# Chunks 2 and 3 of the gated up-projection: from two ordinary products each to a first seven-product pair that shares its time with the making of the sums of x

## The chip, the core and the metric

The kernel runs on one core of one Trainium2 chip. The metric is the device time of one execution in microseconds (us), from the kernel's start to its end. All matrices are fp32; the matrix engine works on them as pairs of a rounded high part (fp32r) and the rest, its low part, so one product of two fp32 matrices is three matrix multiplications: high by high, high by low, low by high.

Engines, as the profile names them: PE (matrix multiplications), PEld (its weight loads), ACT (ScalarE), DVE (VectorE), POOL (GpSimd), SP (it only issues DMAs here). Each takes its instructions in the order in which the program gives them, so an instruction that waits holds up all that stand behind it on its engine.

## The reference

Two decoder layers over x (512 tokens of 1024 features). Each layer has an attention part and then a gated feed-forward part; only the latter is touched:

```python
def conv_ffn(xn, w_up, cw, cb, w_down):        # xn: (1, 512, 1024), w_up: (1024, 5632)
    a = xn @ w_up
    T = a.shape[1]
    ap = jnp.pad(a, ((0, 0), (CONV_W - 1, 0), (0, 0)))
    a = sum(ap[:, j:j + T] * cw[j] for j in range(CONV_W)) + cb
    gate, val = jnp.split(a, 2, axis=-1)
    return (jax.nn.gelu(gate, approximate=True) * val) @ w_down
...
f = conv_ffn(rms_norm(h, g[2]), w_up[l], conv_w[l], conv_b[l], w_down[l])
h = h + rms_norm(f, g[3])
```

w_up has 2816 gate columns and 2816 value columns: 22 chunks of 128 of each. A chunk c is finished by three conv taps on gate and value, a GELU and a product.

## The kernel before

The function `ffn` (line 616) does one layer's feed-forward part, with x transposed (features on the partitions, 512 tokens along the row) and split in high (`xT[0]`, two tiles of four feature blocks) and low (`xT[1]`). It is written as one sequence of calls; that sequence is the order on every engine. There is no other scheduler. Its parts in the up-projection:

- `first_products` (L544) makes chunks 0 and 1 (four outputs "first"): the first half of the tokens (LO) for all four while the last two token blocks are still being normed and transposed (`bd.transpose`, L359 to L367), then the second half (HI).
- `sums_in` (L656) makes sums of quarters of x. POOL adds high and low to whole x in two instructions (L660), DVE makes four differences (L662, L663, L665, L666), and ACT and DVE split the results in high (`xsh`, L671) and low (`xsl`, L672). The first tile of sums is called XA, the second XB. It is a generator: each `next` gives out one step.
- Chunks 2 and 3 are ordinary: `up` (L963) multiplies a piece of 1024 x 128 weights by all 512 tokens, 24 matmuls of 512 columns; gate and value of two chunks are four such pieces, 96 matmuls.
- Chunks 4 to 19 go in eight pairs of chunks (class `Pair`, L678, and the loop at L1020). A pair's 1024 x 256 block of gate or value weights is cut in quarters A11, A12, A21, A22, and by Strassen's scheme in the form of Winograd the pair's eight quarter products become seven, of 24 matmuls of 256 columns each: p_1 (A11 by x itself), p_2 (A12 by x), p_3 (S4 by x), p_4 (A22 by XB), p_5 (S1 by XA), p_6 (S2 by XB) and p_7 (S3 by XA). The sums of weights are S1 = A21 + A22, S3 = A11 - A21, S2 = S1 - A11 and S4 = A12 - S2 (`add`, L686, on DVE). The eighth, needless product is what is saved. In the loop a pair's order on PE is p_7, p_6, p_4, p_5, then p_1 of the next pair, then p_2, p_3.

An operand of weights is split by `high` (L703): ACT copies the high part (L705); then either `low` (L710) lets DVE subtract (S2, S3, S4), or, with `added`, ACT also writes the negated weights, rounded the same way (L707), and a DMA that POOL issues adds the raw weights onto them (L708), which leaves the low part. PE multiplies the low weights as the third matmul of each group of three (L288, L289, L290 in `mm3`), so it stops there if the low part is late.

`keep` (L725) copies partial results out of PSUM on ACT, `Chunk.tap` (L632) runs the conv taps on ACT (L623) and DVE (L624, L625), `gelu` is L643, `product` L645. Weights come by SP's queue in the order of the list `pieces` (L150), made by `add_ffn` (L182); `W.ahead` and `W.ahead_dma` say how many pieces ahead are split and loaded.

Before the change, the program stands after `first_products` as: POOL's two additions, taps of chunk 0, the differences, product of chunk 0, taps of chunk 1, chunk 2's two products with the splitting of the sums, S1 and S3 beside them, chunk 3's two products with S2, S4 and A22, then p_1 of pair 4 and the loop.

Of the kernel before, what the change touches and what calls it, by code (L numbers as in the profile page):

```python
# [13 lines left out]
ALU = mybir.AluOpType  # L14
# [4 lines left out]
KD = D // 128  # L19
HD = 64  # L20
DFF = 2816
# [3 lines left out]
BIG = 3.0e38  # L25


PAIRS = tuple(range(4, 20, 2))
ND = NF // 2
LAST = 3  # L30

# [84 lines left out]
def trunk_kernel(ctx, tc, x, norm_gains, w_qkv_a, w_o_a, w_q_b, w_o_b, kv_norm, w_kvf, b_f,  # L116
# [11 lines left out]
    def t8(shape, dt=F32, name="t8"):  # L128
        return p8.tile(shape, dt, tag="t8", name=name)
# [52 lines left out]
    def add_ffn(l):  # L182
        for c in range(NF):
            if c in PAIRS:
                for q, f in ((0, 0), (0, DFF), (1, DFF), (1, 0)):
                    add_block(w_up[l], q, f + c * 128)
            elif c - 1 not in PAIRS:
                add_cols(w_up[l], c * 128)
                add_cols(w_up[l], DFF + c * 128)

        for j in range(ND):
            add(lambda raw, j=j: [(raw[:, 0:512], w_down[l][j * 256:j * 256 + 128, 0:512]),
                                  (raw[:, 512:1024], dT[l][j, :, 0:512])])
            add(lambda raw, j=j: [(raw, dT[l][j, :, 512:1536])])
        add_rows(w_down[l], range(1, NF, 2))
# [345 lines left out]
                self.out(b)  # L541


    def first_products(bd, n):  # L544
        bd.norm(3)
        outs = [bank([128, T], name="first") for _ in range(n)]
        ws = []
        for i, o in enumerate(outs):
            ws.append(W.get())
            feat_mm(ws[i], bd.xT, o, LO)  # L550
            if i == 0:
                bd.transpose(2)
            if i == 2:
                bd.transpose(3)
        for w, o in zip(ws, outs):
            feat_mm(w, bd.xT, o, HI)
        return outs
# [58 lines left out]
    def ffn(l, bd, cp, nxt, gain, ahead):  # L616
# [39 lines left out]
        def sums_in():  # L656

            v = [t8([128, 4, T], name=f"xsum{i}") for i in range(2)]
            for i in range(2):
                pool.tensor_tensor(v[i], xT[0][i].bitcast(F32), xT[1][i].bitcast(F32), ALU.add)  # L660
            yield
            dve.tensor_tensor(v[0][:, :, LO], v[0][:, :, HI], v[0][:, :, LO], ALU.subtract)  # L662
            dve.tensor_tensor(v[0][:, :, HI], v[1][:, :, HI], v[0][:, :, HI], ALU.subtract)  # L663
            yield
            dve.tensor_tensor(v[1][:, :, HI], v[1][:, :, HI], v[0][:, :, LO], ALU.subtract)  # L665
            dve.tensor_tensor(v[1][:, :, LO], v[1][:, :, LO], v[1][:, :, HI], ALU.subtract)  # L666
            yield
            for X, src in ((XA, v[0]), (XB, v[1])):
                X += [t8([128, 4, T], F32R, name="xsh"), t8([128, 4, T], F32R, name="xsl")]
                for k in (0, 2):  # L670
                    act.copy(X[0][:, k:k + 2], src[:, k:k + 2])  # L671
                    dve.tensor_tensor(X[1][:, k:k + 2], src[:, k:k + 2], X[0][:, k:k + 2].bitcast(F32), ALU.subtract)  # L672
                    yield
# [211 lines left out]
        def run(steps):  # L885
            for _ in steps:
                pass
# [78 lines left out]
                bh, bl = xs(xT, kc, ALL)  # L966
                mm3(o, wh[:, kc, :], wl[:, kc, :], bh, bl, kc == 0, kc == KD - 1)

        base = W.n_get
        first = first_products(bd, 4)  # L970
        xT = bd.xT
        extra = sums_in()
        next(extra)
        done, last = Chunk(0, first[0:2]), Chunk(1, first[2:4])
        done.taps()
        next(extra)
        done.product()
        last.taps()
        W.ahead, W.ahead_dma = 1, 3
        W.split(base + 7)  # L980
        W.high_added()
        pairs = [Pair(c) for c in PAIRS]
        p, n = pairs[0:2]

        banks = p.new_banks()
        up(W.get(), banks[0], range(KD))
        for _ in range(3):
            next(extra, None)
        p.take("A11", "A21", "A22")
        p.high("A11", True)  # L990
        p.s1()
        p.s3()
        up(W.get(), banks[1], range(KD))
        run(extra)
        p.high("S1", True)
        done, last = last, Chunk(2, banks)

        banks = p.new_banks()
        up(W.get(), banks[0], range(KD))
        done.product()  # L1000
        last.tap(0)
        p.high("S3")
        p.s2()
        last.tap(1)
        p.high("S2")
        last.gelu()
        p.take("A12")
        p.low("S3")
        p.s4()
        up(W.get(), banks[1], range(KD))  # L1010
        p.high("A22", True)
        p.low("S2")
        last.product()
        n.take("A11")
        n.high("A11", True)
        p.p_1()
        p.keep_1()
        prev, m = None, [Chunk(3, banks)]

        for i, p in enumerate(pairs):  # L1020
            W.n_get += 4
# [3 lines left out]
            if prev:  # L1025
                prev.sum_1()
            a.tap(0)
            p.high("A12", True)
            p.keep_7()
            p.p_6()  # L1030
            a.tap(1)
            if n:
                n.take("A21", "A22")
                n.s1()
            else:
                W.high_added()
# [25 lines left out]
                b.gelu()  # L1062
            if n:
                n.high("S1", True)
            p.p_2()
            if n:
                n.s2()
            if prev:
# [17 lines left out]
            prev, m = p, p.chunks()  # L1086
# [820 lines left out]
```

## Time and profile before

| what | value |
|---|---|
| device time, median of 3 runs | 1103.73 us (1103.61 to 1103.82) |
| the profiled execution's own time | 1104.32 us |
| its span, first to last instruction | 1102.5 us |
| mean granted PE clock | 0.998 |
| DVE busy | 892.3 us (81%) |
| ACT busy | 735.1 us (67%) |
| POOL busy | 231.5 us (21%) |

Layer 0's feed-forward part begins with `first_products` at 178.0 us of the span, layer 1's at 759.8 us. A row of the timeline gives the start, the length, engine, line, operation, output and inputs with buffer numbers left out, the shape, how many equal instructions are merged (x2), and in brackets how long the engine had been idle and what ended that. A row of the windows gives a stretch, and each engine's busy time in it with the number of instructions that touch it. Pipelined instructions overlap a little, so what one costs in a row is the distance from its start to the next start.

### The profile page before, as it was taken

How to read it: one execution, taken by the hardware profiler on the slowest of the kernel's cores; microseconds unless marked ns; L12 is line 12 of the kernel's file. 1: busy time of each engine (PE TensorE's matmuls, PEld its weight loads, DVE VectorE, ACT ScalarE, POOL GpSimd, SP SyncE). 2: the span in 40 equal slices, each digit the busy share in tenths (PEclk: the TensorE clock that was granted, in tenths of full speed). 3: DMA queues.
4: the chain of work that ended last, by engine and by line, in shares of the span. 5: the costliest groups of instructions: out<-in, count | busy, mean ns of one | idle time of the engine just before them, and what ended most of it. 6: DMA issues, size and time to landing. Idle time of an engine off the chain costs nothing.

```text
span 1102.5 us, 18986 instructions
## 1 busy us (share of the span) xinstructions
PE 1093.6 (99%) x6905; PEld 968.5 (88%) x6905; DVE 892.3 (81%) x1453; ACT 735.1 (67%) x1232; POOL 231.5 (21%) x335
## 2 busy tenths in 40 slices
PE   9999999999999999999999999999999999999997
PEld 6988889899999988888878888889999999988886
DVE  5897788967887789997698677868967887789994
ACT  6754575777788766576562588856677787856572
POOL 2632001322122211000000545600412122211000
PEclk9999999999999999999999999999999999999999
DMA  9699855499999999793447666783499999998872
GB/s 325 184 356 410 317 174 151 91 227 231 224 224 248 230 295 325 277 338 101 134 153 268 210 159 169 216 265 117 98 224 231 231 221 247 224 296 313 317 249 76
DMA packets 156006, 252.06 MB, mean 229 GB/s; under 512 B 12352, under 2 KB 99384, under 8 KB 155912
## 3 DMA queue, kind: packets, MB, share of 16 engines
q1 hardware_dynamic: 137576, 186.61, 51.1%
q0 software_dynamic: 18336, 64.24, 26.3%
q8 instruction: 54, 0.88, 0.3%
q14 instruction: 40, 0.33, 0.1%
HBM read 166.08 MB, written 39.63 MB: 187 GB/s over the span
## 4 chain that ended last, share of the span: by engine, by line
PE 85%; issue 9%; DVE 2%; ACT 2%; DMA 1%; POOL 1%; DVEq 0%; SPq 0%; POOLq 0%; ACTq 0%
PE up L288 12%; PE up L289 12%; PE up L290 12%; PE acc L288 8%; PE acc L290 8%; PE acc L289 8%; PE qk_ps L289 2%; PE qk_ps L288 2%; PE qk_ps L290 2%; PE s_ps L1733 2%; PE o_ps L1781 2%; PE pT_ps L1766 1%; PE first L290 1%; PE first L288 1%; PE first L289 1%
## 5 line engine op out<-in xcount | busy, mean ns | idle before, releaser
L288 PE MATMUL up<-xsh,w 128*128 128x256 f32 x512 | 144.9, 283 | 0.0
L289 PE MATMUL up<-xsl,w 128*128 128x256 f32 x512 | 144.9, 283 | 0.0
L290 PE MATMUL up<-xsh,w 128*128 128x256 f32 x512 | 144.9, 283 | 0.0
L288 PE MATMUL acc<-w 128*128 128x512 f32 (+1 forms) x311 | 120.7, 388 | 0.3 <-DVE mix L337 0.3
L290 PE MATMUL acc<-w 128*128 128x512 f32 (+1 forms) x311 | 120.6, 388 | 0.1
L705 ACT CAST w<-wraw 128x1024 fp32r<-128x1024 f32 x80 | 82.6, 1048 | 37.7 <-DVE wraw L689 37.7
L624 DVE SCALAR_TENSOR_TENSOR bb<-up,conv,bb 128x511 f32<-128x511 f32 x80 | 59.8, 748 | 57.2 <-ACT bb L623 57.0
L289 PE MATMUL acc<-w 128*128 128x512 f32 (+1 forms) x267 | 103.2, 387 | 0.0
L288 PEld LDWEIGHTS up<-xsh,w 128*128 128x128 f32 x512 | 98.3, 192 | 0.0
L289 PEld LDWEIGHTS up<-xsl,w 128*128 128x128 f32 x512 | 98.3, 192 | 0.0
L290 PEld LDWEIGHTS up<-xsh,w 128*128 128x128 f32 x512 | 98.3, 192 | 0.0
L623 ACT ACTIVATE bb<-up,conv 128x512 f32<-128x512 f32 x80 | 60.2, 780 | 32.7 <-DVE up L775 24.3
L288 PE MATMUL up<-xbh,w 128*128 128x256 f32 (+1 forms) x256 | 80.0, 312 | 0.1
L288 PE MATMUL up<-xch,w 128*128 128x256 f32 (+1 forms) x256 | 80.0, 312 | 0.1
L289 PE MATMUL up<-xbl,w 128*128 128x256 f32 (+1 forms) x256 | 79.2, 310 | 0.0
L289 PE MATMUL up<-xcl,w 128*128 128x256 f32 (+1 forms) x256 | 79.2, 310 | 0.0
L290 PE MATMUL up<-xbh,w 128*128 128x256 f32 (+1 forms) x256 | 79.2, 309 | 0.0
L290 PE MATMUL up<-xch,w 128*128 128x256 f32 (+1 forms) x256 | 79.2, 309 | 0.0
L708 POOL DMA_DIRECT2D w<-wraw x48 | 40.4, 841 | 183.5 <-ACT w L707 96.5
L76 DVE TENSOR_TENSOR w<-wraw,w 128x1024 fp32r<-128x1024 f32 x48 | 65.0, 1376 | 11.9 <-ACT w L58 11.4
L58 ACT CAST w<-wraw 128x1024 fp32r<-128x1024 f32 x62 | 63.7, 1051 | 15.8 <-PE v_ps L289 6.9
L290 PEld LDWEIGHTS acc<-w 128*128 128x128 f32 x311 | 58.4, 188 | 12.9 <-DVE w L817 0.9
(308 smaller groups left out, 3279.6 us busy)
## 6 DMA issues: line engine op xcount, KB each, us to landing
wraw<-in_w_up_dram SPq DMA_DIRECT2D x88, 512.0 KB, 6.6
w<-wraw POOLq DMA_DIRECT2D x62, 512.0 KB, 7.6
dT<-dsums SPq DMA_DIRECT2D x28, 512.0 KB, 7.5
dsums<-in_w_down_dram SPq DMA_DIRECT2D x22, 512.0 KB, 7.5
dsums<-in_w_down_dram SPq DMA_DIRECT2D x44, 256.0 KB, 6.6
hD<-hc POOLq DMA_DIRECT2D x44, 256.0 KB, 7.3
wraw<-dT SPq DMA_DIRECT2D x22, 512.0 KB, 6.8
dact<-hD SPq DMA_DIRECT2D x44, 256.0 KB, 5.3
```

The lines of the kernel that those rows point to most:

```text
L58: self.nc.scalar.copy(pair[:, 0], raw)
L76: self.nc.vector.tensor_tensor(pair[:, 1], raw, pair[:, 0].bitcast(F32), ALU.subtract)
L288: pe.matmul(o, ah, bh, start=first, stop=False, skip_group_check=shared)
L289: pe.matmul(o, ah, bl, start=False, stop=False, skip_group_check=shared)
L290: pe.matmul(o, al, bh, start=False, stop=last, skip_group_check=shared)
L623: act.activation(bb[:, s, :], ps, AF.Identity, bias=cp[:, 3, ch:ch + 1], scale=cp[:, 2, ch:ch + 1])
L624: dve.scalar_tensor_tensor(bb[:, s, 1:], ps[:, :T - 1], cp[:, 1, ch:ch + 1], bb[:, s, 1:], ALU.mult, ALU.add)
L705: act.copy(w[:, 0], self.f[key])
L708: pool.dma_start(w[:, 1], self.f[key], accum_op=ALU.add)
L1733: pe.matmul(s[hh][:, :nn], qT[j][:, m, hh, i * 128:(i + 1) * 128], k, start=m == 0, stop=m == 1)
L1766: pe.transpose(o[:, k0 + k, :], p[:, hh, k * 128:(k + 1) * 128], ident)
L1781: pe.matmul(o[64 * hh:64 * hh + 64, i * 128:(i + 1) * 128], Vt[hd // 8][:, k, (hd % 8) * 64:(hd % 8) * 64 + 64], pT[j, i, hh][:, k, :], st ...
```

## The change

`PAIRS` now begins with 2: chunks 2 and 3 become a ninth pair in each layer, and `add_ffn` lists that pair's quarters as A11, A12, A21, A22 (the other pairs keep A11, A21, A22, A12). The four pieces of 96 matmuls of 512 columns become seven products, 168 matmuls of 256 columns. The order around them is rewritten:

- `first_products` splits no weights ahead any more. After the second output it calls `begin`, which takes A11 and A12 and gives out A11's splitting.
- `sums_in` makes XB's two differences only after XA is split.
- After `first_products`: POOL's additions, then A12's splitting, S1 and S3 on DVE, taps of chunk 0, S3's high part, S2, XA's differences, product of chunk 0, p_1, S3's low part, XA's splitting, S2's high part, XB's differences and splitting, S2's low part, p_2, keep_1. Chunk 1's taps move into the loop, to the first pair.
- In the loop the first pair has no p_2 between the next pair's p_1 and its own p_3, gives out A22 and S4 after the first tap, and S1 and the next pair's A11 after the second.

```diff
-PAIRS = tuple(range(4, 20, 2))
+PAIRS = tuple(range(2, 20, 2))
...
-                for q, f in ((0, 0), (0, DFF), (1, DFF), (1, 0)):
+                blocks = (0, 0), (0, DFF), (1, DFF), (1, 0)
+                for q, f in blocks if c > PAIRS[0] else (blocks[0], blocks[3], *blocks[1:3]):
...
             if i == 0:
+                W.ahead, W.ahead_dma = 1, 2
                 bd.transpose(2)
+            if i == 1:
+                begin()
...
-            dve.tensor_tensor(v[1][:, :, HI], v[1][:, :, HI], v[0][:, :, LO], ALU.subtract)
-            dve.tensor_tensor(v[1][:, :, LO], v[1][:, :, LO], v[1][:, :, HI], ALU.subtract)
-            yield
             for X, src in ((XA, v[0]), (XB, v[1])):
+                if src is v[1]:
+                    dve.tensor_tensor(src[:, :, HI], src[:, :, HI], v[0][:, :, LO], ALU.subtract)
+                    dve.tensor_tensor(src[:, :, LO], src[:, :, LO], src[:, :, HI], ALU.subtract)
+                    yield
...
+        pairs = [Pair(c) for c in PAIRS]
+        p = pairs[0]
+
+        def begin():
+            p.take("A11", "A12")
+            p.high("A11", True)
+
+        first = first_products(bd, 4, begin)
         xT = bd.xT
-        extra = sums_in()
-        next(extra)
+        sums = sums_in()
+        next(sums)
+        p.high("A12", True)
+        p.take("A21", "A22")
+        p.s1()
+        p.s3()
         done, last = Chunk(0, first[0:2]), Chunk(1, first[2:4])
         done.taps()
...
+        p.high("S3")
+        p.s2()
+        next(sums)
+        done.product()
+        p.p_1()
+        p.low("S3")
+        for _ in range(2):
+            next(sums)
+        p.high("S2")
+        for _ in range(3):
+            next(sums)
+        p.low("S2")
+        p.p_2()
+        p.keep_1()
+        W.ahead_dma = 3
+        prev, m = None, [last]
...
             a.tap(0)
-            p.high("A12", True)
+            if prev:
+                p.high("A12", True)
+            else:
+                p.high("A22", True)
+                p.s4()
             p.keep_7()
             p.p_6()
             a.tap(1)
+            if not prev:
+                p.high("S1", True)
+                n.take("A11")
+                n.high("A11", True)
...
-            p.p_2()
+            if prev:
+                p.p_2()
```

The program's order on two engines shows the moves. All rows are of layer 0; the changed kernel's line numbers are four or five higher. First DVE after the last block of x has been split (`xbl1`): before, the rows from there to chunk 1's first tap. `w_2104` is a weight of chunk 3, `first_1988` and `first_1989` are chunk 0's gate and value, `xsum0` and `xsum1` are the two tiles of sums.

```order
L367 TENSOR_TENSOR xbl1_1861<-xt_ps_2093,xbh1_1859 128x4x128
L76 TENSOR_TENSOR w_2104<-wraw_2030,w_2104 128x1024
L624 SCALAR_TENSOR_TENSOR bb_2231<-first_1988,conv_1687,bb_2231 128x511
L625 SCALAR_TENSOR_TENSOR bb_2231<-first_1988,conv_1687,bb_2231 128x510
L624 SCALAR_TENSOR_TENSOR bb_2231<-first_1989,conv_1687,bb_2231 128x511
L625 SCALAR_TENSOR_TENSOR bb_2231<-first_1989,conv_1687,bb_2231 128x510
L662 TENSOR_TENSOR xsum0_2227<-xsum0_2227 128x4x256
L663 TENSOR_TENSOR xsum0_2227<-xsum1_2228,xsum0_2227 128x4x256
L650 TENSOR_TENSOR hc_2241<-bb_2231 128x512
L624 SCALAR_TENSOR_TENSOR bb_2243<-first_1990,conv_1687,bb_2243 128x511
```

And the same place of DVE now, from the same split to S3's low part; the two L694 rows that come first are S1 and S3, the third is S2.

```order
L368 TENSOR_TENSOR xbl1_1861<-xt_ps_2091,xbh1_1859 128x4x128
L694 TENSOR_TENSOR wsum_2232<-wraw_2054,wraw_2056 128x1024
L694 TENSOR_TENSOR wraw_2054<-wraw_1740,wraw_2054 128x1024
L628 SCALAR_TENSOR_TENSOR bb_2235<-first_1988,conv_1687,bb_2235 128x511
L629 SCALAR_TENSOR_TENSOR bb_2235<-first_1988,conv_1687,bb_2235 128x510
L628 SCALAR_TENSOR_TENSOR bb_2235<-first_1989,conv_1687,bb_2235 128x511
L629 SCALAR_TENSOR_TENSOR bb_2235<-first_1989,conv_1687,bb_2235 128x510
L694 TENSOR_TENSOR wraw_1740<-wsum_2232,wraw_1740 128x1024
L666 TENSOR_TENSOR xsum0_2220<-xsum0_2220 128x4x256
L667 TENSOR_TENSOR xsum0_2220<-xsum1_2221,xsum0_2220 128x4x256
L654 TENSOR_TENSOR hc_2248<-bb_2235 128x512
L717 TENSOR_TENSOR w_2243<-wraw_2054,w_2243 128x1024
```

One subtraction with both inputs in SBUF (L76) has become two (L694), and S2 now stands between the taps and the differences of x; chunk 1's taps are gone from here.

On ACT, before, the rows that split the sums of x and the first operands of pair 4: `w_2299` is A11, `w_2336` S1, `w_2373` S3, and `up_2259` and `up_2260` are chunk 2.

```order
L671 CAST xsh_2287<-xsum0_2227 128x1024 x2
L705 CAST w_2299<-wraw_2102 128x1024
L707 ACTIVATE w_2299<-wraw_2102 128x1024
L671 CAST xsh_2330<-xsum1_2228 128x1024 x2
L705 CAST w_2336<-wsum_2303 128x1024
L707 ACTIVATE w_2336<-wsum_2303 128x1024
L623 ACTIVATE bb_2369<-up_2259,conv_1687 128x512
L705 CAST w_2373<-wraw_2251 128x1024
```

And now, from S2's high part (`w_2283`) to S1's splitting (`w_2387`); `xsh_2287` is XB, `w_2351` is A22, `up_2250` and `up_2251` hold p_1, `up_2321` and `up_2322` hold p_7, `first_1990` and `first_1991` are chunk 1.

```order
L710 CAST w_2283<-wraw_1740 128x1024
L676 CAST xsh_2287<-xsum1_2221 128x1024 x2
L733 COPY csum_2318<-up_2250 128x256
L733 COPY csum_2318<-up_2251 128x256
L627 ACTIVATE bb_2347<-first_1990,conv_1687 128x512
L710 CAST w_2351<-wraw_2056 128x1024
L712 ACTIVATE w_2351<-wraw_2056 128x1024
L733 COPY csum_2357<-up_2321 128x256
L733 COPY csum_2357<-up_2322 128x256
L627 ACTIVATE bb_2347<-first_1991,conv_1687 128x512
L710 CAST w_2387<-wsum_2232 128x1024
L712 ACTIVATE w_2387<-wsum_2232 128x1024
```

The two casts of the first pair's A22 now stand behind the casts of XB, two copies and a tap, and S1's behind two more copies and another tap.

40 lines of the change are left out of this document (1 added, 39 removed).

## The prediction

> **What bounds the kernel now.** I read the page first (busy times, the chain that ended last), then the waits of PE.
>
> ```profile
> PE 1093.6 (99%) x6905; PEld 968.5 (88%) x6905; DVE 892.3 (81%) x1453; ACT 735.1 (67%) x1232; POOL 231.5 (21%) x335
> PE 85%; issue 9%; DVE 2%; ACT 2%; DMA 1%; POOL 1%; DVEq 0%; SPq 0%; POOLq 0%; ACTq 0%
> PE warm L248 <- DVE zero L243: 1.2, 1, 1.2
> PE qk_ps L289 <- DVE w L80: 0.3, 1, 0.3
> ```
>
> PE is busy for 99% of the span, and its longest wait is 1.2 us, at the start; the next is 0.3. So nothing later can take up a delay: each microsecond by which PE has less to do is won, and each by which it stands still is lost. The change touches one stretch of each layer, so I went on to the windows of that stretch in layer 0, chunks 2 and 3 first, then pair 4 as a whole pair in the running loop (the counts include two neighbours that touch the edges, so 96 and 168 are the products' own).
>
> ```profile
> core 0: us, PE busy (x), PEclk, DMA share, GB/s
> 202.76:224.55 21.79, 21.79 (x98) 1.00 0.65 144
> 227.42:247.58 20.16, 20.16 (x170) 1.00 0.98 244
> ```
>
> **The change part by part.** *The product count.* 96 matmuls of 512 columns take 21.79 us; a pair's 168 of 256 columns take 20.16, which is 0.12 us a matmul and 2.88 us for each of the seven products. The gain is 1.63 us a layer, if no product waits. It is the only gain there is: 3.3 us in two layers.
>
> *The cover.* Before, 21.79 + 2.88 us of products lay between the last product of `first_products` (202.76) and the first one that needs sums of x. Now only p_1 and p_2 do, 5.76 us, so XA and S3 must be there by 202.76 + 5.76 = 208.5, and XB and S2 by 211.4. What makes them is a chain on DVE, whose rows before are these (taps L624 and L625, differences L662 to L666, splitting L672, sums of weights L689):
>
> ```profile
> 188.76 1.29 DVE L367 TENSOR_TENSOR xbl<-xt_ps,xbh 128x512 fp32r<-128x512 f32 x2 [0.88 <-ACT xbh L366]
> 190.19 5.04 DVE L76 TENSOR_TENSOR w<-wraw,w 128x1024 fp32r<-128x1024 f32 x1
> 195.15 0.74 DVE L624 SCALAR_TENSOR_TENSOR bb<-first,conv,bb 128x511 f32<-128x511 f32 x1
> ...
> 199.47 1.33 DVE L662 TENSOR_TENSOR xsum<-xsum 128x1024 f32<-128x1024 f32 x1
> 200.90 1.23 DVE L663 TENSOR_TENSOR xsum<-xsum,xsum 128x1024 f32<-128x1024 f32 x1
> 202.04 0.69 DVE L650 TENSOR_TENSOR hc<-bb 128x512 f32<-128x512 f32 x1
> 202.65 0.74 DVE L624 SCALAR_TENSOR_TENSOR bb<-first,conv,bb 128x511 f32<-128x511 f32 x1
> ...
> 205.53 1.22 DVE L665 TENSOR_TENSOR xsum<-xsum,xsum 128x1024 f32<-128x1024 f32 x1
> 206.78 1.23 DVE L666 TENSOR_TENSOR xsum<-xsum 128x1024 f32<-128x1024 f32 x1
> 207.93 2.35 DVE L672 TENSOR_TENSOR xsl<-xsum,xsh 128x1024 fp32r<-128x1024 f32 x2
> 210.20 1.22 DVE L689 TENSOR_TENSOR wsum<-wraw 128x1024 f32<-128x1024 f32 x1
> ...
> 212.59 2.35 DVE L672 TENSOR_TENSOR xsl<-xsum,xsh 128x1024 fp32r<-128x1024 f32 x2
> ```
>
> Prices, from start to start: a chunk's four tap instructions 2.88 us (202.65 to 205.53), two differences 2.40 (205.53 to 207.93), one subtraction of 1024 columns 1.15 (2.35 for two), the product `hc` 0.60. L76 is the same operation, and took 5.04 us at 190.19. The cause stands beside it, on POOL:
>
> ```profile
> 189.53 4.62 POOL L660 TENSOR_TENSOR xsum<-xbh,xbl 128x2048 f32<-128x2048 f32 x1 [52.12 <-DVE xbl L367]
> 194.10 5.61 POOL L660 TENSOR_TENSOR xsum<-xbh,xbl 128x2048 f32<-128x2048 f32 x1
> 771.94 5.04 DVE L76 TENSOR_TENSOR w<-wraw,w 128x1024 fp32r<-128x1024 f32 x1
> ```
>
> L76, with both inputs in SBUF, stood still until POOL's first addition ended at 194.1 and then ran its 1.1 us; POOL's second addition is recorded 1.0 us longer than its first, for it waited for L76. The taps, which read one input from PSUM, ran beside POOL at their usual 0.74. In layer 1 (the last row) L76 takes 5.04 us again. In the changed order S1 and S3 stand in L76's place, two such operations, and the second waits for the first, whose input it overwrites. Which of DVE and POOL comes next when both want to go on is shown at 27 to 30 us, where DVE has seven such operations in a row and POOL eight casts:
>
> ```profile
> 25.93 1.10 POOL L1169 CAST xpl<-xal 128x512 fp32r<-128x512 f32 x1
> 28.22 1.31 POOL L1169 CAST xpl<-xal 128x512 fp32r<-128x512 f32 x1
> 28.49 1.33 DVE L80 SCALAR_TENSOR_TENSOR w<-wearly,gcol,w 128x256 fp32r<-128x256 f32 x1
> 29.47 1.29 POOL L1169 CAST xph<-xah 128x512 fp32r<-128x512 f32 x1
> ```
>
> They take turns: a cast that takes 1.10 us alone takes 1.3, and between two casts DVE gets through one instruction, never two. So S1 runs from 194.1 to 195.2, POOL's second addition until 199.7, and S3, in L662's place, until 200.8. Everything behind it on DVE moves: chunk 0's taps, that ended at 199.5, now begin at 200.8 and end at 203.7. Then S2 to 204.85, XA's differences to 207.25, `hc` 207.85, S3's low part 209.0, XA's two low halves 210.2 and 211.35, XB's differences 213.75. ACT and POOL come in here:
>
> ```profile
> 208.60 1.05 ACT L705 CAST w<-wraw 128x1024 fp32r<-128x1024 f32 x1
> 209.55 1.06 ACT L707 ACTIVATE w<-wraw 128x1024 fp32r<-128x1024 f32 x1
> 210.50 2.00 ACT L671 CAST xsh<-xsum 128x1024 fp32r<-128x1024 f32 x2
> 210.91 0.84 POOL L708 DMA_DIRECT2D w<-wraw  x1 [2.89 <-ACT w L707]
> DMA to landing us min/median/max: 5.6/5.6/10.0
> 230.46 0.64 ACT L728 COPY csum<-up 128x256 f32<-128x256 f32 x2
> 230.98 0.81 ACT L623 ACTIVATE bb<-up,conv 128x512 f32<-128x512 f32 x1
> 231.65 1.07 ACT L705 CAST w<-wsum 128x1024 fp32r<-128x1024 f32 x1
> ```
>
> Two casts take 2.0 us, two copies 0.52, a tap 0.67, and from the end of a negation (209.55 + 1.06) to POOL's issue pass 0.3; the landing line, of the six DMAs of L708 between 170 and 240 us, says 5.6 more. So XB's casts end at 215.75 (213.75 + 2.0), its low halves at 217.2 (the second after the second cast, by 1.2 to 1.4), S2's low part at 218.4.
>
> *PE's side.* p_1 starts at 202.76: A11's casts and DMA stand ahead of POOL's additions. p_2 wants A12's low part at 205.9 and has it: its DMA goes out behind the additions at 199.8 and lands by 205.4. p_7 starts its low half at 210.2 and ends about 213.6, 2.2 late. p_6 wants S2's low part in its third matmul, at 211.64 by the dense schedule, and gets it at 218.4: PE is 6.8 us late by then. p_6 ends at 221.05. p_4 wants A22's low part at 221.3. Its casts begin behind XB's, two copies and a tap, at 215.75 + 0.52 + 0.67 = 216.95, end at 219.0, the DMA is issued at 219.3 and lands at 224.9: 3.6 us more. S1, behind two copies, a tap and two casts (222.2), lands at 228.1, and p_5 wants it at 224.9 + 2.88 = 227.8: 0.3. After that I find all in time: the next pair's A11 lands at 230.1 for 231.0, its S3 is ready at 235.4 for 236.7 (DVE must wait for p_5's end, then does the last sum, S2, S4 and that). Loads are no limit: on SP's queue A21 and A22 stand at the places of the pieces that went out at 169 and 175 us:
>
> ```profile
> 169.14 0.37 SPq L48 DMA_DIRECT2D wraw<-in_w_up_dram  x1
> 175.46 0.99 SPq L48 DMA_DIRECT2D wraw<-in_w_up_dram  x2
> ```
>
> *The sum.* Per layer 6.8 + 3.6 + 0.3 = 10.7 us of waiting, less 1.63: 9.1 us; two layers 18.2. The profiled execution took 1104.32 us (span 1102.5), so 1122.5; the median of the three runs is 0.6 lower, so 1121.9 us. The bounds of the uncertain prices: the DMA of A22 lands in 4.6 us (L96, the same DMA, in the row below) to 10.0, which is -1.0 to +4.4 a layer; with S1 behind it, whose own landing shifts alike.
>
> ```profile
> L96 POOL DMA_DIRECT2D w<-wraw x1: 912/912/912, 207.1 to 207.1; - x1
> DMA to landing us min/median/max: 4.6/4.6/4.6
> 1096.70:1098.60 1.90, 0.00 (x0) 1.00 0.00 0
> 1098.70:1102.40 3.70, 0.00 (x0) 0.50 0.38 142
> ```
>
> *The clock.* The last two rows are windows after PE's last matmul (1096.6): the granted clock is 1.00 for two more microseconds, then 0.50. Nowhere else does it fall, since PE nowhere stands still. Now it would, for 4.8 us (213.6 to 218.4, with two matmuls in it) and 3.6 us (221.3 to 224.9). If it falls in the first of these, p_6 takes 5.76 instead of 2.88, but ends at 224.2, before A22 lands: hidden. If the half clock lasts into p_4 or comes from the second stop, one product at half speed costs 2.88 us. My sum leaves it at nothing, since the larger stop's share is hidden.
>
> The Trainium skill ("TensorE: Matmul & The Clock Gate", Part 1) says that PE falls to half its clock after an idle window of about 3.4 us, and rises again after about as long a busy one. By that rule both stops can reach a window; the sum would be a few microseconds more, as in the second rival. Only the end of this trace shows such a fall, after two idle microseconds.
>
> **The rivals.** *S1 and S3 get through early.* If DVE ran both without standing behind POOL's second addition (the order of turns at the end of a long addition is not in this trace for two dependent operations), DVE's chain would start where it did, with the taps done by 199.47. The same list gives XB's differences at 209.5, its casts at 211.5, S2's low part 214.1: 2.5 late. A22 then lands at 211.5 + 0.52 + 0.67 + 2.0 + 0.3 + 5.6 = 220.6, wanted at 214.1 + 2.88 = 217.0: 3.6, and S1 0.4. Together 6.5 - 1.63 = 4.9 a layer, 9.8 in all: 1113.5 us. Against it: the turns above. It shows that the lock on DVE decides half of the loss only; the place of A22 in ACT's order gives the rest.
>
> *The clock falls and shows.* One product a layer at half speed, 2.88 us, on top of the forecast: 1121.9 + 5.8 = 1127.7. For it: the stops are longer than the one after which the clock fell at the end. Against it: the first and longer one is followed by work that A22 hides.
>
> *The cover holds, and it becomes faster.* The mechanism: the chain for XB before, ending at 214.9 (212.59 + 2.35) with chunk 1's taps (2.88) and S1 and S3 (2.4) in it, loses these 5.3 us, which move behind it or into DVE's idle time, and gains S2 and S3's low part (2.3); that puts XB near 212 and S2 near 213. It would need 211.6, and A22 cast by 208.5 so that it lands by 214.5. From these two points on the gain of 3.3 us would show: 1100.4. Against it: ACT casts A22 behind XB, so it cannot be cast by 208.5 in this order; only if PE did not have to wait for that DMA would it hold.
>
> **How the numbers follow.** The forecast has 0.62, early S1 and S3 0.16, the clock 0.14, the cover 0.05; 0.03 is left for what I have not seen. Faster by over 0.2% (about what a measurement of this kernel can tell from no change, 2.2 us) is the last rival: 0.05. Within 0.2% takes a gain and a loss that happen to meet: 0.02 of the unseen. The rest, 0.93, is slower. The range goes from 1112 (the early rival with a quicker landing, 1113.5 less 1.5) to 1128 (the clock, or A22 landing in 8.5 us in both layers).
>
> **What the changed profile would show.** PE idle some 10 us in each of two places, near 203 to 228 us and 785 to 810: first before p_7 ended by DVE `xsl`, then in p_6 by DVE's low part of S2, then in p_4 by the DMA of A22. On DVE one of the two L694 rows after the last xbl lasting about 5 us and the other too. PE's slice digits at these places fall to 5 or 6. Wrong would be: S1 and S3 at 1.2 us each by 193; A22's DMA landing under 4 us after its issue; no idle PE at p_4; or PE idle as told, yet a time that does not rise, which would mean that PE had room later.

## The result and the profile after

| | before | after |
|---|---|---|
| median of the runs, us | 1103.78 (1103.55 to 1104.12) | 1133.18 (1132.01 to 1135.57) |
| profiled execution, us (its span) | 1104.32 (1102.5) | 1132.01 (1130.2) |
| mean granted clock of the profiled execution | 0.998 (whole until PE's last matmul) | 0.989 |

The changed kernel is slower by 2.7%: the ratio is 1.027, with an interval of 1.0256 to 1.0284. The sign was forecast; the time lies 5.2 us above the end of the range (1128.0). One of its six runs (1351.12 us at a clock of 0.75) was disturbed and is left out; the median with it, 1133.81, is the 1133.8 that the expectations below start from.

On the page of the changed kernel, PE's row and the row of its slices:

```profile
PE 1101.0 (97%) x7049; PEld 980.8 (87%) x7049; DVE 914.6 (81%) x1473; ACT 748.0 (66%) x1256; POOL 236.7 (21%) x341
PE   9999999789999999999999999999789999999997
```

PE has two dents, in the two slices from 198 to 254 us and the two from 791 to 848 (7 and 8 tenths), where before it had none. They are shallower than the 5 or 6 forecast, since a slice is 28 us long and PE at half clock counts as busy. Its waits between 195 and 245 us, which is the changed stretch of layer 0 (total, times, longest):

```profile
PE up L291 <- DMA w<-wsum: 4.0, 1, 4.0
PE up L289 <- ACT csum L733: 2.7, 1, 2.7
PE up L290 <- DVE xsl L677: 1.6, 2, 1.4
PE up L291 <- DVE w L717: 1.5, 1, 1.5
PE up L291 <- DMA w<-wraw: 1.2, 1, 1.2
```

In the order of time: p_7 waits for XA's low halves (`xsl`), p_6 for ScalarE's copy and then for S2's low part, p_4 for A22's DMA, and p_5, longest of all, for S1's DMA. They are 11.0 us together. The copy is `keep_1`, which reads p_1's result out of the bank that p_6 adds to:

```profile
215.94 0.64 ACT L733 COPY csum<-up 128x256 f32<-128x256 f32 x2
```

It stands behind XB's casts in ScalarE's order, and p_6 goes on at 216.35, when the first of the two copies is done. Now what stands on VectorE meanwhile (start, duration),

```profile
189.95 5.28 DVE L694 TENSOR_TENSOR wsum<-wraw 128x1024 f32<-128x1024 f32 x1
195.27 5.52 DVE L694 TENSOR_TENSOR wraw<-wraw 128x1024 f32<-128x1024 f32 x1
...
203.59 1.22 DVE L694 TENSOR_TENSOR wraw<-wsum,wraw 128x1024 f32<-128x1024 f32 x1
...
215.12 2.36 DVE L677 TENSOR_TENSOR xsl<-xsum,xsh 128x1024 fp32r<-128x1024 f32 x2 [1.45 <-ACT xsh L676]
217.39 1.22 DVE L717 TENSOR_TENSOR w<-wraw,w 128x1024 fp32r<-128x1024 f32 x1
```

and GpSimd, with the two additions and then the DMAs of A22, of S1 and of the next pair's A11:

```profile
189.53 10.18 POOL L664 TENSOR_TENSOR xsum<-xbh,xbl 128x2048 f32<-128x2048 f32 x2 [2.44 <-DVE xbl L368]
...
219.44 0.84 POOL L713 DMA_DIRECT2D w<-wraw  x1 [18.93 <-ACT csum L733]
222.54 0.83 POOL L713 DMA_DIRECT2D w<-wsum  x1 [2.26 <-ACT w L712]
224.43 0.84 POOL L713 DMA_DIRECT2D w<-wraw  x1 [1.06 <-ACT w L712]
```

The first two rows on VectorE are S1 and S3, both stretched to over 5 us beside GpSimd's additions, as forecast. Behind them come chunk 0's taps from 200.7, S2 from 203.6, XB's low halves until 217.5 and S2's low part until 218.6. How long the DMAs of A22 and of S1 took from issue to landing, and the loads of weights on SP's queue between 212 and 226 us:

```profile
L713 POOL DMA_DIRECT2D w<-wraw x1: 842/842/842, 219.4 to 219.4; - x1
DMA to landing us min/median/max: 5.2/5.2/5.2
L713 POOL DMA_DIRECT2D w<-wsum x1: 832/832/832, 222.5 to 222.5; - x1
DMA to landing us min/median/max: 9.2/9.2/9.2
L48 SPq DMA_DIRECT2D wraw<-in_w_up_dram x2: 368/820/1272, 221.2 to 221.7; - x2
```

A22 took 5.2 us, S1 9.2; two loads of 512 KB went out 1.3 and 0.9 us ahead of S1. Last the windows of the stretch (busy time of PE, granted clock, DMA share, GB/s):

```profile
215.70:222.40 6.70, 4.53 (x19) 0.50 0.26 49
222.50:232.60 10.10, 4.91 (x39) 1.00 1.02 223
232.70:236.10 3.40, 3.40 (x18) 0.50 1.03 248
241.74:261.90 20.16, 20.16 (x169) 1.00 0.91 227
836.73:856.89 20.16, 20.16 (x169) 1.00 0.93 221
```

The clock was halved twice in layer 0, for 6.8 and for 3.4 us, and likewise in layer 1 (from 812.95 and 826.60). The last two rows are the next pair, dense again, in layers 0 and 1. It begins at 241.74 where before it began at 227.42, which is 14.3 us later; in layer 1 it begins at 836.73 where before it began at 809.17, 27.6 us later, so that stretch loses 13.2 us more. The sum is all but 0.1 of the 27.7 us between the two profiled executions. So the whole loss of this execution, the fastest of the five, lies in the stretch that the change touches.

### The profile page after: what moved, and what is told of

The parts are those of the page before. It is cut to its first block, busy times and chain, and to the rows that moved or that the text cites. A ratio compares the mean times of both kernels' runs of the same rounds, so it can differ in the third digit from the quotient of the medians.

```text
span 1130.2 us, 19340 instructions
## 1 busy us (share of the span) xinstructions
PE 1101.0 (97%) x7049; PEld 980.8 (87%) x7049; DVE 914.6 (81%) x1473; ACT 748.0 (66%) x1256; POOL 236.7 (21%) x341
## 4 chain that ended last, share of the span: by engine, by line
PE 89%; issue 6%; DMA 2%; DVE 1%; ACT 1%; POOL 1%; DVEq 0%; POOLq 0%; ACTq 0%
PE up L289 11%; PE up L291 11%; PE up L290 11%; PE acc L289 8%; PE acc L291 8%; PE acc L290 8%; PE qk_ps L290 2%; PE qk_ps L289 2%; PE qk_ps L291 2%; PE v_ps L289 2%; PE v_ps L291 2%; PE v_ps L290 2%; PE s_ps L1730 2%; PE o_ps L1778 2%; DMA w<-wsum 2%
## 5 line engine op out<-in xcount | busy, mean ns | idle before, releaser
L291 PE MATMUL up<-xsh,w 128*128 128x256 f32 x576 | 167.0, 290 | 12.3 <-DMA w<-wsum 7.2
L289 PE MATMUL up<-xsh,w 128*128 128x256 f32 x576 | 166.5, 289 | 5.2 <-ACT csum L733 5.2
L290 PE MATMUL up<-xsl,w 128*128 128x256 f32 x576 | 166.4, 289 | 3.1 <-DVE xsl L677 3.1
L291 PEld LDWEIGHTS up<-xsh,w 128*128 128x128 f32 x576 | 113.7, 197 | 13.6 <-DMA w<-wsum 7.6
L289 PEld LDWEIGHTS up<-xsh,w 128*128 128x128 f32 x576 | 113.8, 198 | 5.6 <-ACT csum L733 5.6
L290 PEld LDWEIGHTS up<-xsl,w 128*128 128x128 f32 x576 | 113.9, 198 | 3.9 <-DVE xsl L677 3.9
L713 POOL DMA_DIRECT2D w<-wraw x54 | 45.5, 842 | 306.9 <-ACT w L712 220.5
L289 PE MATMUL up<-xbh,w 128*128 128x256 f32 (+1 forms) x248 | 74.5, 300 | 0.1
L289 PE MATMUL up<-xch,w 128*128 128x256 f32 (+1 forms) x248 | 74.3, 300 | 0.0
L291 PE MATMUL up<-xch,w 128*128 128x256 f32 (+1 forms) x248 | 73.6, 297 | 0.0
L290 PE MATMUL up<-xcl,w 128*128 128x256 f32 (+1 forms) x248 | 73.6, 297 | 0.0
L290 PE MATMUL up<-xbl,w 128*128 128x256 f32 (+1 forms) x248 | 73.6, 297 | 0.0
L291 PE MATMUL up<-xbh,w 128*128 128x256 f32 (+1 forms) x248 | 73.5, 296 | 0.0
L291 PEld LDWEIGHTS acc<-w 128*128 128x128 f32 x311 | 58.4, 188 | 12.7 <-DVE w L822 0.9
L289 PEld LDWEIGHTS acc<-w 128*128 128x128 f32 x311 | 58.4, 188 | 12.4 <-DVE mix L338 0.7
```

Of the source, the lines that this page charges most:

```text
L289: pe.matmul(o, ah, bh, start=first, stop=False, skip_group_check=shared)
L290: pe.matmul(o, ah, bl, start=False, stop=False, skip_group_check=shared)
L291: pe.matmul(o, al, bh, start=False, stop=last, skip_group_check=shared)
L713: pool.dma_start(w[:, 1], self.f[key], accum_op=ALU.add)
```

## The experiments

Each is timed beside runs of the kernel before on the same chip (their medians lie between 1103.94 and 1104.04). Ratios are to those.

**S1 and S3 early.** All four blocks are taken in `begin()`, and S1 and S3 are made there, in VectorE's idle time ahead of the last block of x, so that neither meets GpSimd's additions.

```diff
-            p.take("A11", "A12")
+            p.take("A11", "A12", "A21", "A22")
             p.high("A11", True)
+            p.s1()
+            p.s3()
...
-        p.take("A21", "A22")
-        p.s1()
-        p.s3()
```

> The changed kernel with S1 and S3 of the first pair made before the last block of x is split, in DVE's idle time, so that neither stands behind POOL's additions. Theory (the stand behind POOL starts the chain on DVE 5 us late): S2's low part comes near 214 us of the span instead of 218.6, the first pair loses about 2.5 + 3.6 us in p_6 and p_4 and something in p_5; 1114 to 1118 us, the upper end if the clock falls once a layer. Rival (the stand does not matter, since A22's and S1's DMAs end last anyway): within 4 us of the changed kernel's 1133.8.

Measured: 1124.79 us (1123.93 to 1125.75), ratio 1.0188 (1.0173 to 1.0204): 8.4 us less, and less than expected. On VectorE the two sums took 1.2 us each, and S2 came at 199.4, 4.2 us earlier:

```profile
185.41 1.22 DVE L694 TENSOR_TENSOR wsum<-wraw 128x1024 f32<-128x1024 f32 x1
186.66 1.23 DVE L694 TENSOR_TENSOR wraw<-wraw 128x1024 f32<-128x1024 f32 x1
```

So the stretch of S1 and S3 is real, and it is worth its 4.2 us a layer. The rest missed because S1's DMA took as long as in the changed kernel, 9.1 us from 218.3 to 227.5, behind two loads that went out at 217.0 and 217.4, and p_5 waited 4.0 us for it again. The clock was also halved twice in each layer, for 3.4 us each time. My expectation had only "something" for p_5, and one such fall a layer at most.

**A22 and S1 split early.** A22 is cast right behind A12, S1 right behind chunk 0's taps; VectorE's order stays.

```diff
         p.high("A12", True)
         p.take("A21", "A22")
+        p.high("A22", True)
...
         done.taps()
+        p.high("S1", True)
         p.high("S3")
...
-                p.high("A22", True)
...
-                p.high("S1", True)
```

> The changed kernel with A22 and S1 split early: A22's two casts stand right behind A12's on ACT, S1's behind chunk 0's GELU, so that both DMAs go out before 208 us. S1 and S3 still stand behind POOL. Theory (their late DMAs cost 3.6 us by the working, 5.2 by the changed trace, in p_4 and p_5): PE waits only in p_7 and p_6, S2's low part still comes at 218.6; without a fall of the clock 1114, with p_6 and p_4 at half clock 1117 to 1121. Both DMAs should land in 4.6 to 6 us, since no loads run beside them. Rival (S1's long landing is the DMA's own, not its neighbours'): S1 lands 9 us after its issue here too.

Measured: 1119.45 us (1118.28 to 1120.42), ratio 1.0139 (1.0124 to 1.0154): as expected. Both waits for DMAs are gone, and S1's DMA (206.2 to 211.9) took 5.7 us, with the loads going out behind it, from 207.0 on. The second fall of the clock is gone with the waits in both layers; one a layer is left, in p_6. This is worth 13.7 us, more than the lock on VectorE.

**Both.** The two edits together.

> Both edits together. Theory: PE waits once, about 2.5 us in p_6 for XB and S2, less 1.6 us of the smaller product count: 0.9 us a layer, 1104 to 1108 us. Rival (one of the two causes is not one): the time of the better of the two single edits.

Measured: 1108.54 us (1108.16 to 1109.96), ratio 1.0044 (1.0027 to 1.006): 0.5 us above what I had expected. What is left of PE's waits between 195 and 245 us, but for 0.4 us at p_6's start:

```profile
PE up L291 <- DVE w L717: 1.8, 1, 1.8
```

p_6 waits for S2's low part, which VectorE still makes behind XB's low halves; in layer 0 it then runs at half clock, from 213.9 to 217.3 us. So 24.6 of the 29.4 us come from where four steps stand in two engines' orders, with the falls of the clock that this brings.

**The clock kept up.** The changed kernel with matmuls that nobody reads in the first pair's three stops.

```diff
+        def idle(k):
+            o = bank([128, T], name="idle")
+            for _ in range(k):
+                pe.matmul(o, xT[0][0][:, 0, 0:128], xT[0][0][:, 0, :], start=True, stop=True)
...
             p.keep_7()
+            if not prev:
+                idle(16)
             p.p_6()
```

(likewise `idle(12)` ahead of p_4 and `idle(14)` ahead of p_5)

> The changed kernel, its waits left as they are, but PE does matmuls in them whose result nobody reads (16 ahead of p_6, 12 ahead of p_4, 14 ahead of p_5 of the first pair, 3.6, 2.7 and 3.2 us). They add work and take no wait away. Theory (the granted clock falls to a half because PE stands still, and the second fall costs 1.7 us a layer in p_5 and the next p_1, while the first is hidden behind A22's DMA): the granted clock stays at 1.00 and the time falls by 3 to 4 us, to about 1130. Rival (the half clock costs nothing, or the whole difference to the forecast): no change or more, or 1122.

Measured: 1130.55 us (1129.91 to 1131.4), ratio 1.0241 (1.0226 to 1.0256). In the windows of layer 0 in which the changed kernel ran at half clock, this one ran at the whole:

```profile
215.70:222.40 6.70, 5.54 (x37) 1.00 0.17 31
232.70:236.10 3.40, 3.40 (x30) 1.00 1.06 249
```

The time is 2.6 us less, by the ratios 3.2, and the intervals of the two ratios just touch. The added matmuls cost something themselves: in layer 0 p_6 goes on at 219.37 instead of 218.67 and S1's DMA lands 0.5 us later, and the next pair begins at 240.79 instead of 241.74. One fall was left, in layer 1, at 806.9. So the halved clock costs about 3 us of the 29.4, if anything more. The other 26.8 us stay with the clock kept up.

**S4 later.** S4 frees a buffer, and a load follows at once. Here the first pair makes S4 after p_5 is given out, so that no load goes out just ahead of S1's DMA.

```diff
                 p.high("A22", True)
-                p.s4()
...
             p.p_5()
             p.sum_3()
+            if not prev:
+                p.s4()
+                p.high("S4")
+                p.low("S4")
```

> The changed kernel with S4 of the first pair made after p_5 is given out instead of before p_6. The two loads of weights that go out at 221 us of the changed trace wait for S4, and S1's DMA, issued at 222.5, lands 9.2 us later beside them. Theory (loads that run at the same time lengthen S1's DMA): if the loads go out later than 226, S1 lands in 5.5 to 6.5 us and PE waits 2.5 to 3.5 us less in p_5; 1127 to 1130 us. Rival (the length comes from the DMAs of its own queue, A22's before it and the next pair's A11 behind it): S1 still lands after 9 us, and the time stays at 1132 to 1136.

Measured: 1130.87 us (1130.76 to 1131.11), ratio 1.0245 (1.0229 to 1.026). S1's DMA, and the only load between 212 and 230 us:

```profile
L713 POOL DMA_DIRECT2D w<-wsum x1: 832/832/832, 222.2 to 222.2; - x1
DMA to landing us min/median/max: 5.6/5.6/5.6
...
L48 SPq DMA_DIRECT2D wraw<-in_w_up_dram x1: 368/368/368, 223.6 to 223.6; - x1
```

With no load ahead of it the DMA takes 5.6 us instead of 9.2 (5.3 instead of 8.4 in layer 1), which shows the cause. The time fell by 2.3 us only, and ends 0.9 us above the range that I had expected: p_5's wait fell from 4.0 to 1.1 us, but the next pair's A11, issued at 224.1 behind that load, took 8.8, and its p_1 waited 2.0 us for it.

**The next pair's A11 later.** Its split is moved behind p_5, to see whether that DMA slows S1's.

> The changed kernel with the splitting of the next pair's A11 moved from before p_4 to behind p_5, so that its DMA is issued some microseconds after S1's instead of 1.9 after it. Looked at for S1's landing: with the loads as the cause it stays near 9 us; with the DMAs of its own queue as the cause it falls to 5.5 to 6.5 us. The next p_1 may then wait for A11, so the time itself tells little.

Measured, in one round: 1135.54 us, ratio 1.0287 (1.0268 to 1.0305), no better. S1's DMA took 9.5 us, with the two loads at 221.2 and 221.6 as before. A transfer that goes out after S1's does not slow it; the two ahead of it do.

**All in time.** Everything that p_4 to p_7 need is moved up: S1, S3 and the splits of A11, A12, A22 and S1 early, S2 behind XA's differences, its low part ahead of XB's; chunk 0's taps, GELU and product behind p_2.

```diff
         next(sums)
-        p.high("A12", True)
...
+        p.high("A22", True)
+        p.high("S1", True)
         p.high("S3")
+        next(sums)
         p.s2()
-        next(sums)
-        done.product()
         p.p_1()
...
         p.high("S2")
-        for _ in range(3):
+        p.keep_1()
+        next(sums)
+        p.low("S2")
+        for _ in range(2):
             next(sums)
-        p.low("S2")
         p.p_2()
-        p.keep_1()
+        done, last = Chunk(0, first[0:2]), Chunk(1, first[2:4])
+        done.taps()
+        done.product()
```

> A version that should beat both: S1 and S3 of the first pair made in DVE's idle time before the last block of x is split, A12 split there too, A22, S1 and S3 split on ACT right after, chunk 0's taps moved behind XB's splitting and S2, keep_1 before XB's casts. Theory (nothing but those places makes PE wait, and the count of matmuls is worth 1.63 us a layer): no wait over 0.5 us in the first pair, granted clock 1.00 throughout, 1100 to 1101.5 us against 1103.9 before. Rival (a cause is missing, XB still late in p_6): 1103 to 1107.

Measured: 1110.43 us (1109.76 to 1111.27), ratio 1.006 (1.0048 to 1.0073): a miss, and no better than the version with both edits. The clock stayed whole and p_6 waited for nothing, but new waits came. PE's, from 195 to 245 us:

```profile
PE up L289 <- ACT csum L733: 2.5, 2, 1.6
PE up L291 <- DMA w<-wraw: 1.7, 1, 1.7
```

and ScalarE's rows ahead of the first of them:

```profile
213.03 1.28 ACT L647 ACT_TABLE_LOAD   x1 [1.62 <-DVE bb L629]
214.32 0.63 ACT L647 ACTIVATE bb<-bb 128x512 f32<-128x512 f32 x1
...
215.52 0.63 ACT L733 COPY csum<-up 128x256 f32<-128x256 f32 x2
```

The copy `keep_7`, which p_4 needs, stands behind chunk 0's GELU, that is behind a wait for VectorE's taps and a table load; `keep_2` stood behind a cast of S4, and the next pair's A11 was issued too late.

**The three orders mended.** On top of the last: the GELU and product of chunk 0 behind p_4, S4 right behind XB's low halves, the next pair's A11 split right behind `keep_1`.

```diff
         p.keep_1()
+        pairs[1].take("A11")
+        pairs[1].high("A11", True)
...
+        p.s4()
         done, last = Chunk(0, first[0:2]), Chunk(1, first[2:4])
-        done.taps()
-        done.product()
+        done.tap(0)
+        done.tap(1)
...
             p.p_4()
+            if not prev:
+                done.gelu()
+                done.product()
             a.gelu()
```

> This is the version with all in time, with the three orders mended that its waits named: chunk 0's GELU and its product stand behind the giving out of p_4 instead of ahead of keep_7, S4 is made right behind XB's low parts instead of behind chunk 0's taps, and the next pair's A11 is split right behind keep_1. In that version TensorE stopped for 1.61, 0.93 and 1.69 us in layer 0 and for 1.64, 0.92 and 1.13 us in layer 1, 7.9 us in all, of its 1110.4. My theory (the pair's waits are orders and transfers alone, and the sums and the products themselves cost nothing more): all six go, the clock stays whole, and the time is 1110.4 - 7.9 = 1102.5, between 1100.5 (the forecast's gain of 3.3 us whole) and 1103.5. The rival (the engines beside TensorE have no room for the pair's steps here, so that a wait mended is a wait elsewhere): 1105 to 1110, with new stops of over 2 us a layer.

Measured: 1108.85 us (1107.99 to 1109.57), ratio 1.0044 (1.003 to 1.0058): a miss, as the rival had it. The three waits are gone; these took their place (PE, 195 to 250 us, the longest two groups):

```profile
PE up L289 <- DVE up L775: 1.7, 2, 1.2
PE up L291 <- DVE w L717: 0.5, 1, 0.5
```

The first is p_3 waiting for `sum_4`: VectorE rests for 0.3 us in all between 199.8 and 230 here and comes to it late. It had idled for 4.2 us until 193.95, since its first difference waited for GpSimd's first addition; that difference then took 5.6 us beside the second addition, and not 1.2.

**The additions on VectorE.** The changed kernel, with the two additions of `sums_in` moved from GpSimd to VectorE.

```diff
-                pool.tensor_tensor(v[i], xT[0][i].bitcast(F32), xT[1][i].bitcast(F32), ALU.add)
+                dve.tensor_tensor(v[i], xT[0][i].bitcast(F32), xT[1][i].bitcast(F32), ALU.add)
```

> The changed kernel with one edit: VectorE makes the two additions of the sums of x that GpSimd made (10.18 us on POOL from 189.53, VectorE's S1 and S3 stretched to 5.28 and 5.52 us beside them). My theory (S1 and S3 stand behind GpSimd's additions and push the taps of chunk 0, S2 and all that makes the sums back): from rows of 1024 elements in 1.2 us the two additions of 2048 take about 4.6 us on VectorE, so S1 and S3 end near 197 instead of 200.8, S2 begins near 200 instead of 203.59, and the whole chain to p_5 moves 3.4 to 3.8 us ahead in each layer; S1's transfer stays slow, since the two loads still run beside it: 1133.8 - 7.2 = 1126.6, between 1124.5 and 1128.5. The rival (VectorE is simply full here, and 4.6 us more of additions on it cost what the lost stretch gives): 1131 to 1137.

Measured: 1123.77 us (1123.4 to 1124.81), ratio 1.0181 (1.0167 to 1.0195): 9.4 us less, and 0.7 us below the range that I had expected.

```profile
190.06 4.48 DVE L664 TENSOR_TENSOR xsum<-xbh,xbl 128x2048 f32<-128x2048 f32 x2
...
195.71 1.22 DVE L694 TENSOR_TENSOR wraw<-wraw 128x1024 f32<-128x1024 f32 x1
```

With the two additions on its own queue VectorE is done with them, S1 and S3 by 196.9 us; with GpSimd's help it took until 200.8. S2 began at 199.7, 3.9 us earlier. S1's DMA still took over 9 us.

**All in time, additions on VectorE.** The mended version with that edit, and S4 made right behind S2.

> The version with all in time and its three orders mended, with two more edits: VectorE makes the two additions of the sums of x, and S4 is made right behind S2, both ahead of XA's low parts. There VectorE had no rest from 199.8 to 230, and TensorE stopped for sum_4 (1.16 us), for the low part of the next pair's S3 (0.48) and for what followed from it (0.32 and 0.52) in layer 0, and alike in layer 1. My theory (what holds that version back is VectorE's queue, which starts too late, because the first differences wait for GpSimd's second addition until 194.1 and the stretch leaves it idle for 4.2 us ahead of that): the queue runs about 3.5 us earlier, the four stops go, and the time is 1100.5 to 1102.5, below the kernel before for the first time. The rival (the seven-product pair needs more of VectorE than there is, so that the stops only move): 1104 to 1109.

Measured: 1106.39 us (1106.18 to 1107.2), ratio 1.0022 (1.0013 to 1.0032): a miss, with the number in the rival's range. VectorE now rested for 1.7 us ahead of 210.2 and for 1.5 ahead of 218.7, but I had also put `keep_1` behind XB's casts, and p_2 stood still for it in each layer; the second, smaller stop is p_3's for `sum_4`, on VectorE, as before:

```profile
PE up L289 <- ACT csum L733: 1.6, 1, 1.6
PE up L289 <- DVE up L775: 0.5, 1, 0.5
```

**Its two stops out, and the control.** `keep_1` ahead of XB's casts again, and the second pair's `sum_4` ahead of the second tap of chunk 3; beside it the kernel before with VectorE making the additions.

```diff
         p.high("S2")
+        p.keep_1()
         next(sums)
...
-        p.keep_1()
         pairs[1].take("A11")
...
+            if i == 1:
+                p.sum_4()
             if prev:
                 b.tap(1)
...
-            p.sum_4()
+            if i != 1:
+                p.sum_4()
```

> The last version with its two stops a layer taken out: ScalarE copies keep_1 ahead of XB's casts again (behind them it held p_2 up by 1.80 us in each layer), and the second pair's sum_4 stands ahead of the second tap of chunk 3 (behind it, it held p_3 up by 0.62 us). My theory (the first pair costs its matmuls and its stops and nothing else): 1106.4 - 2 x (1.80 + 0.10 + 0.62 + 0.10) = 1106.4 - 5.2 = 1101.2, between 1100.3 and 1102.2, which is faster than the kernel before by 0.15 to 0.35%. The rival (some new wait takes the place of these two): 1103 to 1106.

> The kernel before, unchanged but for VectorE making the two additions of the sums of x instead of GpSimd: the control for the versions that carry this edit. My theory (the edit is worth only what TensorE waited for, and TensorE waits for nothing in the up-projection of the kernel before): no difference, 1103.5 to 1104.5. The rival (the edit helps or hurts by itself, with no pair beside it): a difference of over 1.5 us to either side.

Measured: 1102.70 us (1101.59 to 1103.31), ratio 0.9985 (0.9976 to 0.9994), faster than the kernel before by 0.06 to 0.24%, though 1.5 us slower than the 1101.2 expected and 0.5 above that range. The control took 1103.98 us, ratio 0.9998 (0.999 to 1.0007), so the edit of the additions is worth nothing by itself. The faster version's windows in layer 0, first the eight products from the first pair's p_1 to the next pair's, then the next pair from its p_7:

```profile
202.59:225.63 23.04, 23.04 (x195) 1.00 0.52 132
225.63:245.79 20.16, 20.16 (x167) 1.00 1.02 245
```

PE never stands still there. Eight products take 23.04 us, 2.88 each, and the next pair begins at 225.63 instead of 227.42, from a start at 202.59 instead of 202.76: the gain of 1.62 us in this layer is what the prediction had counted for the products. In layer 1 a wait of 0.7 us for a DMA, late in the up-projection at 961 us, takes part of it back, so that the kernel as a whole won 1.2 of the 3.3 us. That wait is not in the kernel before; what causes it was not tried.

## Why the prediction was right in sign and wrong in size

*The products' gain* (1.63 us a layer): right. It shows as soon as nothing waits, and not before.

*The lock, and S1 and S3 standing behind the additions*: right. Forecast were S1 to 195.2, S3 to 200.8, S2's low part at 218.4; the rows end at 195.2, 200.8 and 218.6. The first experiment takes it away and wins 8.4 us, the move of the additions 9.4. The wait of p_6 for `keep_1` was not in the list; S2's low part, which ended later, covered it.

*A22's DMA behind XB's casts* (landing at 224.9): right, it landed at 224.6. p_4's own wait was 1.2 us and not 3.6, since p_6 ran at half clock and used up the difference, as the step on the clock said that it would.

*S1's DMA* (landing at 228.1, a wait of 0.3): this step failed. The mechanism, p_5 waiting for that DMA, was named; its size was not. I took 5.6 us from the landing line of the kernel before, whose own other end was 10.0, and wrote "Loads are no limit". The wait was 4.0 us in layer 0. Two loads had gone out within 1.3 us ahead of the DMA. The kernel before had shown this: its DMA that took 10.0 us went out at 224.12, and these rows say what was ahead of it (256 KB of `hc` went out at 222.5 besides):

```profile
224.12 0.85 POOL L708 DMA_DIRECT2D w<-wraw  x1 [0.71 <-issue]
L48 SPq DMA_DIRECT2D wraw<-in_w_up_dram x2: 368/774/1181, 223.0 to 223.6; - x2
```

Taking the loads away gave 5.6 (S4 later); a DMA taken from behind it changed nothing (the next pair's A11 later). That is 3.6 us in layer 0, and p_5's 3.2 us wait says nearly as much in layer 1.

*The clock* ("My sum leaves it at nothing, since the larger stop's share is hidden"): this step failed too. It was right for the first fall. But S1's longer wait brought a second fall, in p_5 and the next pair's p_1, where nothing hides it: 3.4 us at half speed are 1.7 us of work. The second fall goes when S1 is split early and its wait with it. The experiment that keeps the clock up gives some 3 us for the two layers; the rival had 5.8. The Trainium skill ("TensorE: Matmul & The Clock Gate", Part 1), which I had weighed and set aside, gave the right sign: a few microseconds more.

*The sum.* Per layer 9.1 us forecast; in layer 0 the late DMA adds 3.6 and the second fall 1.7, which makes 14.4, where 14.3 was measured. *The range* held either of the two, since the clock alone was a rival at 1127.7 and a late landing reached 1128, but not both together; and a longer stop can bring the fall with it, so they were not independent.

*The rival that S1 and S3 get through early* (1113.5) carried the same 5.6 us: when the first experiment took the lock away, S1's DMA and two falls of the clock in each layer kept the time at 1124.8.

*The rival that the cover holds* was refused with the right reason for this order: A22 cannot be cast by 208.5. In another order it can, and then the gain shows whole in layer 0. So the loss lies in the order of the steps around the pair. The pair itself brings its 1.6 us in a layer in which nothing waits; in layer 1 that was not reached.

## What to carry to other kernels

When work is taken from in front of a consumer, list what its inputs queue behind on every engine, and move those steps first: here four misplaced steps cost some 25 us, where the change itself can bring 3.3 at most. Take a DMA's time from rows that have the same company: count the loads that go out just ahead of it, since a freed buffer upstream is what sends them. Where PE is to stop for about 2 us out of 3.4, add the halved clock to the sum unless something surely hides it; two stops that depend on each other belong in one case of the range.

## What the runs showed of the hardware

*The clock falls by windows, and half a window of rest is enough.* In the changed kernel the clock falls at 215.62, 232.69, 812.95 and 826.60 us: the distances from the first are 5, 175 and 179 times 3.413 us. Four of the windows of that length, laid on the same grid (busy time of PE in the second column):

```profile
212.21:215.62 3.41, 1.41 (x12) 1.00 0.13 44
222.45:225.86 3.41, 2.21 (x18) 1.00 1.01 223
225.86:229.27 3.41, 1.93 (x17) 1.00 1.02 240
229.27:232.69 3.42, 0.92 (x7) 1.00 1.05 208
```

After the first and the last of them the clock is halved, after the two between it stays whole. Over all these runs, every such window of the stretch with less than 1.6 us of busy time was followed by half clock, and all but one of those with 2.0 us or more by whole clock; between 1.7 and 1.95 both occur. The Trainium skill ("TensorE: Matmul & The Clock Gate", Part 1) gives a free-running window of 3413 ns, which these distances bear out, and calls the window that lowers the clock an idle one; here it was as much as half busy. Where the grid lies differs from trace to trace (the first falls come 0.6, 3.4 and 1.5 us past a multiple of 3.413 us in the changed kernel and the first two experiments), which would also explain why the changed kernel's times spread over 3.6 us and the kernel before's over 0.6; that was not tried by itself.

*A transfer takes longer behind loads that went out just ahead of it.* The same accumulating DMA of 512 KB, for A22 or S1, took 4.5 to 6.1 us with nothing out within 1.8 us ahead of it, 6.5 to 7.3 with one more of its kind out 0.6 us ahead, and 8.4 to 9.8 with two loads of 512 KB out within 1.4 us ahead.

*A stop costs a little more than its gap.* p_2's gap of 1.64 us in the version with the additions on VectorE put its second matmul 1.90 us behind: 0.26 us on top. Of these, 0.16 lie in the record, since a matmul is drawn 0.28 us long while the next starts 0.12 after it; the other 0.10 is that the second follows the first by 0.22 and not by 0.12.

*The slower engine was no help.* GpSimd takes 10.18 us for the two additions, with one turn of VectorE (S1's) between them, and 9.23 in the version with the three orders mended, where none comes between; VectorE takes 4.48.
